# The seam into an attention layer and the attention loop: queues, banks and order of issue rewritten, with the arithmetic kept

## The chip, the core and the metric

The kernel runs on one core of a Trainium2 chip. The metric is device time in microseconds (us) of one execution. The core has a matrix engine (PE in the profile, with its weight loads shown as PEld), a vector engine (DVE), a scalar engine (ACT), a general engine (POOL) and a queue that only issues transfers and waits (SP). Matrix products land in PSUM, which has eight banks of 128 x 512 numbers in single precision; everything else lives in SBUF or in the memory outside the core, and transfers (DMAs) move between the two.

## The reference, cut to what matters

A decoder trunk of two layers over 1024 positions and 1024 features: a recurrent mixer, a feed-forward layer, stick-breaking attention with 16 heads of 64, a second feed-forward layer, and norms between them. The change touches the end of the first feed-forward layer, the norm before attention, and attention itself:

```python
def rms_norm(x, g):
    y = xf * lax.rsqrt(jnp.mean(xf * xf, axis=-1, keepdims=True) + RMS_EPS)
...
def stick_breaking_attention(x, w_qkv, w_o):
    qkv = jnp.einsum("bsd,de->bse", x, w_qkv).reshape(bsz, seq, 3, N_HEADS, HEAD_DIM)
...
        z = jnp.einsum("bhqd,bhkd->bhqk", qb, kb) * scale
        strict = s_idx < t_idx
        log_fail = jnp.where(strict, jax.nn.log_sigmoid(-z), 0.0)
        suffix = lax.cumsum(log_fail, axis=3, reverse=True) - log_fail
        weights = jnp.where(strict, jnp.exp(jax.nn.log_sigmoid(z) + suffix), 0.0)
        outs.append(jnp.einsum("bhqk,bhkd->bhqd", weights, vb))
...
    return jnp.einsum("bse,ed->bsd", o, w_o)
```

A weight of attention is thus sigmoid(z) times the product of sigmoid(-z) over all later keys up to the query, which the kernel forms with a scan along the row instead of logarithms and sums.

## The kernel before, in words

Every large product is made of three matmuls (`mm3`, L141 to L143): both operands are split into a high part in a rounded format and a low part, and high x high, high x low and low x high are added up in PSUM.

**The seam.** The last stage of the feed-forward layer visits output rows d in the order of `VISITS`. The last two visits finish the row pairs (3, 7) and (0, 4). For each finished row and half n of the positions, `finished` (L1035) stores h, calls `prep` (L214: the high part on ACT, the low part on DVE) and `squares` (L207: a square on ACT, an add onto `rbc[n]` on DVE). Then attention starts: the first q projection runs on PE, while `stats` turns the sums of squares into columns with matmuls, `rstd` makes factors of them (one ACT square root, five small DVE operations) and `broadcast_r` spreads these over a PSUM bank, which DVE copies to `rbc[n]`.

**The projections.** `qkv_steps(q)` is a generator. For pair of heads q it makes three projections (`which` 0 to 2 for q, k, v) of two halves n with eight `mm3` each, and gives control back after each `mm3`. A finished group is multiplied by `rbc[n]` on DVE (`t`, L1337). For q and k, ACT copies the high part to `qh_`, DVE makes the low part `ql_`, and SP copies the halves of these to the tiles `q`, `kh` and `kl` by transfers of 128 KB. For v, `v_turn` transposes `t` on PE in one of the two banks of `psQ` and splits it with two ACT copies and two DVE subtractions. `next_weights` splits the next projection's weights: one ACT copy of 128 x 1024 at once, and two DVE halves put on the list `later`.

**The attention loop.** Its unit is an iteration u (from -8 to 191). An iteration makes: `z_part` of chunk u + 8 (two matmuls for scores, in the two banks of `psZ`); `t_part` and `t_split` of unit u + 2 (transposes of finished weights in the two banks of `psT`, high part `th` on ACT, low part `tl` on DVE); `z_rest` of the chunk (two sigmoids on ACT, the scan on DVE, the product on POOL); one entry of `later`; two steps of the filling work (`fill`: the projections of the next pair, and after the last pair the first products with w_o into the tile `ob`); and `av_part` of unit u (two matmuls into a bank of `psO`). A head has 12 chunks: rows 0 to 7 on the diagonal (L1412), then rows 4 to 7 against the first 512 keys (L1414), whose scan starts with the last value of the diagonal's scan, kept in its tile `F4` to `F7`. A finished sum of a head is taken from PSUM by `gather`, and a pair's result is split and stored outside by `parts`; both are appended to `later`.

**What sets the order.** PE, ACT, DVE and POOL execute the order in which the code is written (`manual_schedule`). In attention the order of SP's queue is set by the framework's planner. Each engine takes its own list strictly in order, and the SP queue does too.

**The end.** After the last v projection, `all_fill` brings the stored results back from outside to `xh` and `xl` (L1495, L1496), makes the last turn of v, gives up `psQ`, opens `ob` in its place and fills in products with w_o.

Of the kernel before, what the change touches and what calls it, by code (L numbers as in the profile page):

```python
# [16 lines left out]
P = 128  # L17
# [16 lines left out]
def trunk(  # L34
# [562 lines left out]
    def mix_out_ffn_in(h, mix, bias, layer, gnext, ob):  # L597
# [124 lines left out]
        with tc.manual_schedule(engines={E.PE, E.Activation, E.DVE, E.Pool}):  # L722
# [309 lines left out]
            begun_sq = set()  # L1032
            done = []

            def finished(d, n):  # L1035
                if final:
                    squares(h, d, n, rbc, acc, first=n not in begun_sq)
                    gain(h, d, n)
                else:
                    nc.sync.dma_start(hd[d][n], h[d][n])  # L1040
                    prep(h, d, n, gnext)
                    squares(h, d, n, acc, rbc, V, first=n not in begun_sq)
                begun_sq.add(n)
# [241 lines left out]
    with ExitStack() as st:  # L1285
# [11 lines left out]
        Q, KH, KL, VV = {}, {}, {}, {}  # L1297
# [5 lines left out]
        late, later = [], []  # L1303

        def next_weights(raw):
            hi, lo = wtile("whi"), wtile("wlo")
            nc.scalar.copy(hi, raw)
            for i in range(NH):
                later.append(lambda c=half(hi, i), a=half(lo, i), b=half(raw, i): nc.vector.tensor_sub(a, b, f32(c)))
# [5 lines left out]
        def qkv_steps(q):  # L1315
            full = lambda tag: [ap.tile([P, S], F32R, tag=tag, name=tag, bufs=4) for _ in range(2)]
            VV[q] = ap.tile([P, NT, 2, P], F32R, tag="v", name="v", bufs=2)
            for which in range(3):
                w = wq.pop((q, which))
                nx = (q, which + 1) if which < 2 else (q + 1, 0)  # L1320
                if nx[0] < NP:
                    wq[nx] = next_weights(load_raw(cols(w_qkv, nx[1] * D + nx[0] * P), (ND,)))
                else:
                    mix[0].load(0)
                    mix[0].w[mix[0].order[0]] = next_weights(mix[0].raw.pop(0))
                    mix[0].load(1)
                    mix[0].load(2)
                for n in range(NH):
                    ps = psQ.tile([P, NB], F32, tag="qk", name="qk_ps")
                    for k in range(ND):  # L1330
                        mm3(ps, w[0][:, k], w[1][:, k], xh[k][n], xl[k][n], k == 0, k == ND - 1)
                        if k == 3 and late:
                            late.pop()()
                        if k < ND - 1:
                            yield
                    t = ap.tile([P, NB], F32, tag="t", name="t", bufs=2)
                    nc.vector.tensor_mul(t, ps, rbc[n])  # L1337
                    cs = slice(n * NB, (n + 1) * NB)
                    if which == 0 and n == 0:
                        Q[q] = full("q")  # L1340
                    if which == 1 and n == 0:
                        KH[q], KL[q] = full("kh"), full("kl")
                    if which < 2:
                        th = ap.tile([P, NB], F32R, tag="qh_", name="qh_", bufs=1)
                        tl = ap.tile([P, NB], F32R, tag="ql_", name="ql_", bufs=1)
                        nc.scalar.copy(th, t)
                        nc.vector.tensor_sub(tl, t, f32(th))
                        move = lambda dst, p0, src, p1: nc.sync.dma_start(f32(dst)[p0, cs], f32(src)[p1])
                        for hx, (a, b) in enumerate(((top, bot), (bot, top))):
                            if which == 0:  # L1350
                                move(Q[q][hx], a, th, a)
                                move(Q[q][hx], b, tl, a)
                            else:
                                for dst, src in ((KH[q][hx], th), (KL[q][hx], tl)):
                                    move(dst, top, src, a)
                                    move(dst, bot, src, a)
                    else:

                        def v_turn(n=n, t=t):
                            tp = psQ.tile([P, NB], F32, tag="qk", name="vt_ps")  # L1360
                            for i in range(4):
                                nc.tensor.transpose(tp[:, i * P : (i + 1) * P], t[:, i * P : (i + 1) * P], ident)
                            src = tp.rearrange("p (b h c) -> p b h c", b=4, h=2)
                            bs = slice(4 * n, 4 * n + 4)
                            for hx in range(2):
                                nc.scalar.copy(VV[q][:, bs, hx, 0:HD], src[:, :, hx])
                                nc.vector.tensor_sub(
                                    VV[q][:, bs, hx, HD:P], src[:, :, hx], f32(VV[q])[:, bs, hx, 0:HD]
                                )

                        late.append(v_turn)
                    yield
# [9 lines left out]
        F_ = {}  # L1382

        def z_part(q, hx, j, ci, c0, c1, diag):
# [3 lines left out]
            nc.tensor.matmul(ps[:, 0 : c1 - c0], lhsT=lhsT, rhs=KH[q][hx][:, c0:c1], start=True, stop=False)  # L1388
            nc.tensor.matmul(ps[:, 0 : c1 - c0], lhsT=lhsT, rhs=KL[q][hx][:, c0:c1], start=False, stop=True)  # L1389
# [202 lines left out]
```

## Time and profile before

| what | value |
|---|---|
| median of three runs | 2208.05 us (2204.42 to 2208.51) |
| the profiled execution's own time | 2209.81 us |
| its span, from first to last instruction | 2207.9 us |
| granted PE clock, mean over the span | 0.994 |
| the seam and attention in the span | from about 957 to about 1479 us |
| one pair of heads in the loop | about 60.5 us |

The profile is one execution. Its tables give busy time by engine, groups of equal instructions, what ended each idle time, and stretches of the span with the clock granted to PE. A start time is counted in us from the first instruction. The end of a matmul is modelled, so consecutive matmuls overlap in the records; the spacing of their starts tells the true pace.

### The profile page before, as it was taken

To read this page: it belongs to the slowest core of one execution; us is meant where nothing else is said; L and a number is where in the kernel's file an instruction comes from. 1 tells how busy PE (TensorE), PEld (TensorE's weight loads), DVE (VectorE), ACT (ScalarE), POOL (GpSimd) and SP (SyncE) were. 2 spreads that over 40 slices of the span, in tenths; PEclk is the share of its full clock that TensorE was granted. 3 is DMA by queue.
4 is the path that set the end of the run, shared out by engine and by line. 5 is a ranking of instruction groups with operands and counts; after the bars stand their busy time and mean duration, and the time that the engine had idled before them with its cause. 6 is when DMAs were issued, how large, how long until landed. Compare 5 with 4: busy or idle time off the path is not lost.

```text
span 2207.9 us, 28478 instructions
## 1 busy us (share of the span) xinstructions
PE 2176.5 (99%) x10120; PEld 1805.7 (82%) x10120; DVE 1709.9 (77%) x2383; ACT 1150.2 (52%) x2007; POOL 287.2 (13%) x379
## 2 busy tenths in 40 slices
PE   7999999999999999999999999989999999999998
PEld 6888888888888888878888888878888888888887
DVE  6887778767777887878888888876876777788876
ACT  5577435343444544546666666653533444454556
POOL 2222020000000000003334333321000000000002
PEclk9999999999999999999999999989999999999999
DMA  7111412334444764444333333532133444467442
GB/s 230 48 48 39 134 39 72 102 123 158 143 149 134 261 209 122 148 136 98 89 94 96 105 87 104 177 128 70 39 110 124 148 148 133 154 225 234 137 152 86
DMA packets 298702, 277.72 MB, mean 126 GB/s; under 512 B 16312, under 2 KB 215104, under 8 KB 298560
## 3 DMA queue, kind: packets, MB, share of 16 engines
q1 hardware_dynamic: 298544, 275.91, 40.1%
q8 instruction: 79, 1.29, 0.2%
q14 instruction: 63, 0.52, 0.1%
q10 hardware_dynamic: 16, 0.00, 0.0%
HBM read 175.71 MB, written 74.97 MB: 114 GB/s over the span
## 4 chain that ended last, share of the span: by engine, by line
PE 88%; DVE 6%; ACT 3%; DMA 1%; issue 1%; SPq 1%; DVEq 0%; ACTq 0%
PE p_ps L143 18%; PE p_ps L141 18%; PE p_ps L142 18%; PE qk_ps L143 3%; PE qk_ps L141 3%; PE qk_ps L142 3%; PE wt_ps L1426 3%; PE ob_ps L142 2%; PE ob_ps L141 2%; PE ob_ps L143 2%; PE a_ps L143 2%; PE a_ps L142 2%; PE a_ps L141 2%; PE z_ps L1388 1%; DVE F L1414 1%; PE z_ps L1389 1%
## 5 line engine op out<-in xcount | busy, mean ns | idle before, releaser
L1415 POOL TENSOR_TENSOR w<-w,F 128x128 f32<-128x128 f32 (+1 forms) x192 | 183.7, 957 | 311.1 <-DVE F L1412 159.0
L143 PE MATMUL p_ps<-vh,wcl 128*128 128x512 f32 x524 | 204.2, 390 | 0.5 <-DVE wcl L682 0.5
L143 PE MATMUL p_ps<-vh,wbl 128*128 128x512 f32 x524 | 204.4, 390 | 0.3 <-DVE wbl L672 0.2
L143 PE MATMUL p_ps<-vh,wal 128*128 128x512 f32 x524 | 204.1, 389 | 0.1
L141 PE MATMUL p_ps<-vh,wbh 128*128 128x512 f32 x524 | 204.2, 390 | 0.0
L141 PE MATMUL p_ps<-vh,wch 128*128 128x512 f32 x524 | 204.1, 389 | 0.0
L142 PE MATMUL p_ps<-vl,wbh 128*128 128x512 f32 x524 | 203.9, 389 | 0.0
L142 PE MATMUL p_ps<-vl,wch 128*128 128x512 f32 x524 | 203.9, 389 | 0.0
L141 PE MATMUL p_ps<-vh,wah 128*128 128x512 f32 x524 | 203.9, 389 | 0.0
L142 PE MATMUL p_ps<-vl,wah 128*128 128x512 f32 x524 | 203.9, 389 | 0.0
L668 ACT CAST wbh<-sb 128x1024 fp32r<-128x1024 f32 (+2 forms) x69 | 69.6, 1009 | 193.7 <-DVE sb L652 193.6
L212 POOL TENSOR_TENSOR acc<-acc,rbc 128x512 f32<-128x512 f32 x30 | 40.4, 1348 | 773.6 <-ACT rbc L211 773.6
L1436 DVE TENSOR_TENSOR tl<-wt_ps,th 128x512 fp32r<-128x512 f32 x192 | 106.0, 552 | 39.2 <-ACT th L1435 37.1
L1435 ACT CAST th<-wt_ps 128x512 fp32r<-128x512 f32 x192 | 92.5, 482 | 83.1 <-PE wt_ps L1426 82.0
L141 PE MATMUL qk_ps<-vh,whi 128*128 128x512 f32 x264 | 118.6, 449 | 0.7 <-ACT vh L215 0.7
L143 PEld LDWEIGHTS p_ps<-vh,wbl 128*128 128x128 f32 x524 | 98.3, 188 | 22.3 <-DVE wbl L672 2.0
L143 PEld LDWEIGHTS p_ps<-vh,wcl 128*128 128x128 f32 x524 | 98.4, 188 | 21.9 <-DVE wcl L682 1.6
L143 PEld LDWEIGHTS p_ps<-vh,wal 128*128 128x128 f32 x524 | 98.4, 188 | 21.3 <-DVE wal L663 1.0
L142 PEld LDWEIGHTS p_ps<-vl,wah 128*128 128x128 f32 x524 | 98.4, 188 | 20.6
L142 PEld LDWEIGHTS p_ps<-vl,wch 128*128 128x128 f32 x524 | 98.4, 188 | 20.5
L142 PEld LDWEIGHTS p_ps<-vl,wbh 128*128 128x128 f32 x524 | 98.4, 188 | 20.5
L141 PEld LDWEIGHTS p_ps<-vh,wbh 128*128 128x128 f32 x524 | 98.4, 188 | 20.3 <-ACT ta L1053 0.2
(400 smaller groups left out, 5851.2 us busy)
## 6 DMA issues: line engine op xcount, KB each, us to landing
raw<-in_ffn_w_in SPq DMA_DIRECT2D x88, 512.0 KB, 3.8
vl<-pd SPq DMA_DIRECT2D x128, 256.0 KB, 3.6
pd<-U SPq DMA_DIRECT2D x90, 256.0 KB, 2.3
raw<-in_ffn_w_out SPq DMA_DIRECT2D x56, 256.0 KB, 3.9
raw<-in_attn_w_qkv SPq DMA_DIRECT2D x24, 512.0 KB, 3.8
raw<-in_lru_w_in SPq DMA_DIRECT2D x16, 512.0 KB, 4.1
acc<-pd SPq DMA_DIRECT2D x28, 256.0 KB, 2.6
pph<-rbc SPq DMA_DIRECT2D x28, 256.0 KB, 2.5
```

What stands on the lines that cost most here:

```text
L141: nc.tensor.matmul(ps, lhsT=wh, rhs=mh, start=first, stop=False, **kw)
L142: nc.tensor.matmul(ps, lhsT=wh, rhs=ml, start=False, stop=False, **kw)
L143: nc.tensor.matmul(ps, lhsT=wl, rhs=mh, start=False, stop=last, **kw)
L212: (eng or nc.gpsimd).tensor_add(acc[n], acc[n], sq)
L668: nc.scalar.copy(self.full(self.wb), self.full(self.sb))
L1388: nc.tensor.matmul(ps[:, 0 : c1 - c0], lhsT=lhsT, rhs=KH[q][hx][:, c0:c1], start=True, stop=False)
L1389: nc.tensor.matmul(ps[:, 0 : c1 - c0], lhsT=lhsT, rhs=KL[q][hx][:, c0:c1], start=False, stop=True)
L1414: nc.vector.tensor_tensor_scan(rev, rev, rev, first, op0=ALU.mult, op1=ALU.bypass)
L1415: nc.gpsimd.tensor_mul(wt, wt, F[:, 1 : n + 1])
L1426: nc.tensor.transpose(tp[:, c : c + P], W[q, hx, j, kb // 4][:, (kb % 4) * P : (kb % 4 + 1) * P], ident)
L1435: nc.scalar.copy(th[:, q0:], tp[:, q0:])
L1436: nc.vector.tensor_sub(tl[:, q0:], tp[:, q0:], f32(th)[:, q0:])
```

## The change

PE, DVE, ACT and POOL keep their arithmetic; PE has the same number of matmuls. What differs is order, buffers and transfers:

1. The squares of the rows of the last two visits (eight of them) leave `finished` and follow, sorted by half, behind the last `prep`.
2. The first two q groups accumulate in `psZ` banks, take the rows in the order 1, 5, 2, 6, 3, 7, 0, 4, and are evacuated only after the factors are there. `stats` and `broadcast_r` stand at fixed steps, and the loop starts after 34 steps of projection instead of 32.
3. A k or q group's two parts lie in one tile `two` (two buffers); kh and kl become one tile `kk`, so a k group needs four transfers of 256 KB instead of eight of 128 KB. The multiplication by `rbc` stays at the end of the group; the split and the transfers follow one step later.
4. Weights are loaded one projection earlier, and split by halves on ACT too.
5. SP's queue follows the written order in attention.
6. `gather` goes to the head of `later`. The value that the scan of a later chunk starts with is copied by POOL to a column `sofar`, and all `F` tiles share four buffers.
7. The last turn of v uses a bank of `psT`; the stored results of half 0 of six pairs are brought back eight steps earlier; two steps without work are dropped before `ob`.
8. In two iterations near the end one chunk more is made, so the loop then runs two chunks further ahead.

```diff
@@ the end of the feed-forward layer
+                    if d in (VISITS[-1][0], VISITS[-2][0], VISITS[-1][0] + HK, VISITS[-2][0] + HK):
+                        last_sq.append((d, n))
+                    else:
+                        squares(h, d, n, acc, rbc, V, first=n not in begun_sq)
...
+            last_sq.sort(key=lambda t: t[1])
+            for k, (d, n) in enumerate(last_sq):
+                nc.scalar.square(acc[k % NH], h[d][n])
+                V.tensor_add(rbc[n], rbc[n], acc[k % NH])
@@ weights
-            nc.scalar.copy(hi, raw)
-            for i in range(NH):
-                later.append(lambda c=half(hi, i), a=half(lo, i), b=half(raw, i): nc.vector.tensor_sub(a, b, f32(c)))
+            part_hi = lambda i: nc.scalar.copy(half(hi, i), half(raw, i))
+            part_lo = lambda i: nc.vector.tensor_sub(half(lo, i), half(raw, i), f32(half(hi, i)))
+            def second():
+                part_lo(0)
+                part_hi(1)
+            later.extend((lambda: part_hi(0), second, lambda: part_lo(1)))
@@ qkv_steps
+                ks = (1, 5, 2, 6, 3, 7, 0, 4) if (q, which) == (0, 0) else range(ND)
+                    pool, tag = (psZ, "z") if (q, which) == (0, 0) else (psQ, "qk")
...
+                    ev = evacuate(q, which, n, ps)
+                    if (q, which) == (0, 0):
+                        waiting.append(ev)
+                        yield
+                    else:
+                        next(ev)
+                        yield
+                        next(ev, None)
@@ evacuate
+                two = ap.tile([P, 2, NB], F32R, tag="two", name="two", bufs=2)
+                nc.scalar.copy(two[:, 0], t)
+                nc.vector.tensor_sub(two[:, 1], t, f32(two)[:, 0])
...
+                        for half_ in (top, bot):
+                            nc.sync.dma_start(f32(KK[q][hx])[half_, :, cs], f32(two)[a])
...
+                pool, tag = (psT, "T") if (q, n) == (NP - 1, 1) else (psQ, "qk")
...
+            if q == NP - 1 and n == 0:
+                bring_back(*((p, 0) for p in range(NP - 2)))
@@ chunks
-            F = ap.tile([P, (n if tag != "F" else NB) + 32], F32, tag=tag, name=tag, bufs=1 if tag != "F" else 3)
+            F = ap.tile([P, NB + 32], F32, tag="F", name="F", bufs=4)
-                first = F_[j][:, 0:1]
+                first = sofar[j]
...
+            if diag and j >= 4:
+                nc.gpsimd.tensor_copy(sofar[j], F[:, 0:1])
-            later.append(gather)
+            later.insert(0, gather)
@@ the driving loops
-        with tc.manual_schedule(engines={E.PE, E.Activation, E.DVE, E.Pool}):
+        with tc.manual_schedule(engines={E.PE, E.Activation, E.DVE, E.Pool, E.SP}):
+            between = {
+                12: lambda: stats(rbc[0], psO, "o", 0),
+                16: lambda: stats(rbc[1], psO, "o", 1),
+                17: lambda: broadcast_r(psO, "o", 0),
+                18: lambda: [*waiting[0]],
+                21: lambda: broadcast_r(psO, "o", 1),
+                22: lambda: [*waiting[1]],
+            }
+            for i in range(1, 2 * ND * NH + 3):
+                next(first)
+                if i in between:
+                    between[i]()
+                if i > 4 and later:
+                    later.pop(0)()
+            gains = (len(units) - 28, len(units) - 26)
...
+                if u in gains:
+                    z_rest(z_part(*chunks[c]), *chunks[c])
+                    c += 1
```

More of the change, by code (lines that the diff above doesn't have):

```diff
@@ L1333, in qkv_steps @@
                             late.pop()()
-                        if k < ND - 1:
+                        if i < ND - 1:
                             yield
[L1336 to L1356, printed above, removed]
-                    else:
[L1359 to L1371, printed above, removed]
```

108 lines of the change are left out of this document (63 added, 45 removed).

## The prediction, as it was put on record

> **What bounds the kernel now.** I read the page first, then PE's waits, then stretches of the span, then single instructions around each wait.
>
> ```profile
> PE 2176.5 (99%) x10120; PEld 1805.7 (82%) x10120; DVE 1709.9 (77%) x2383; ACT 1150.2 (52%) x2007; POOL 287.2 (13%) x379
> PE 88%; DVE 6%; ACT 3%; DMA 1%; issue 1%; SPq 1%; DVEq 0%; ACTq 0%
> ```
>
> PE is busy almost throughout and carries 88% of the chain that ended last. The change leaves PE's work as it is, so it can only win where PE stops. PE's waits between 940 and 1480 us:
>
> ```profile
> PE ob L141 <- issue: 3.9, 1, 3.9
> PE wt_ps L1426 <- DVE tl L1436: 2.7, 2, 1.6
> PE z_ps L1388 <- ACT w L1409: 2.5, 7, 0.4
> PE qk_ps L142 <- DVE vl L216: 0.7, 1, 0.7
> PE qk_ps L141 <- ACT vh L215: 0.7, 1, 0.7
> PE p_ps L143 <- DVE wcl L682: 0.5, 1, 0.5
> PE p_ps L141 <- ACT ta L1053: 0.4, 1, 0.4
> ```
>
> That is 11.4 us in 14 stops: the last four rows are the seam, the third the loop, the first two the end of attention. A stop costs more than its idle time. The stretches, with PE, PEld, DVE, ACT and POOL busy, then PE's clock:
>
> ```profile
> 965.50:970.30 4.80, 3.48 (x15) 2.28 (x13) 4.80 (x9) 4.59 (x7) 0.00 (x0) 1.00 0.78 247
> 970.30:974.90 4.60, 4.60 (x20) 3.78 (x19) 2.39 (x9) 0.45 (x2) 0.69 (x3) 0.63 0.01 4
> 1072.00:1133.00 61.00, 60.63 (x324) 50.97 (x323) 51.53 (x75) 40.51 (x99) 23.74 (x40) 1.00 0.36 96
> 1439.80:1446.00 6.20, 6.20 (x21) 5.28 (x22) 4.86 (x5) 3.52 (x10) 1.09 (x1) 0.52 0.68 192
> 1446.00:1466.80 20.80, 20.80 (x119) 17.82 (x118) 17.83 (x24) 16.17 (x42) 9.59 (x19) 1.00 0.09 27
> 1470.60:1477.00 6.40, 6.40 (x25) 5.34 (x26) 3.09 (x6) 2.38 (x4) 0.80 (x1) 0.54 0.00 0
> 1434.00:1479.00 45.00, 38.38 (x190) 31.78 (x189) 35.75 (x47) 28.46 (x69) 15.53 (x25) 0.85 0.27 89
> ```
>
> After each group of stops the clock is low for 4.6, 6.2 and 6.4 us, at 0.63, 0.52 and 0.54. That loses 4.6 x 0.37 = 1.7, 6.2 x 0.48 = 3.0 and 6.4 x 0.46 = 2.9 us. Besides, the records hide a piece of each stop, since the end of a matmul is modelled:
>
> ```profile
> 1083.66 0.39 PE L142 MATMUL qk_ps<-vl,whi 128*128 128x512 f32 x1
> 1083.88 0.39 PE L143 MATMUL qk_ps<-vh,wlo 128*128 128x512 f32 x1
> 1084.11 0.34 PE L1447 MATMUL av_ps<-th,v 128*128 128x384 f32 x1
> 1084.28 0.34 PE L1448 MATMUL av_ps<-tl,v 128*128 128x384 f32 x1
> 1084.99 0.44 PE L1388 MATMUL z_ps<-kh,q 128*128 128x384 f32 x1 [0.37 <-ACT w L1409]
> ```
>
> A matmul of 512 columns is followed after 0.23 us, one of 384 after 0.17. Here the next starts after 0.71: 0.54 late, for an idle time of 0.37. So each stop costs 0.17 more than its row says.
>
> The rule of the Trainium skill on this ("TensorE: Matmul & The Clock Gate", Part 1) is that the clock halves after an idle window of about 3.4 us. By it the 0.7 us stops of the seam would slow nothing, and the sum below would be 1.7 smaller; the trace has 0.63 right behind them, so I go by the trace.
>
> **Part A, the seam (edits 1, 2).** PE waits because DVE is late with the last low parts:
>
> ```profile
> 968.54 0.69 DVE L212 TENSOR_TENSOR rbc<-rbc,acc 128x512 f32<-128x512 f32 x1
> 969.14 0.75 DVE L216 SCALAR_TENSOR_TENSOR vl<-h,vc,vh 128x512 fp32r<-128x512 f32 x1
> 969.95 0.50 PE L142 MATMUL qk_ps<-vl,whi 128*128 128x512 f32 x1 [0.67 <-DVE vl L216]
> ```
>
> An add of squares takes 0.60 from start to start. Eight of them, 4.8 us, no longer stand between the last h rows and their low parts; they follow, and so do eight squares on ACT. The rows 0 and 4, ready last, are used last: 18 matmuls or 4.1 us into the group. The sums are first needed by the statistics after 12 steps, 36 x 0.23 = 8.3 us, so the moved 4.8 us has cover on DVE. Between statistics of a half and its broadcast lie 5 steps, 3.4 us; the chain of six small operations fits, barely. Removed: 0.7 + 0.7 + 0.5 + 0.4 = 2.3, 4 x 0.17 = 0.7, and the slow clock's 1.7: **-4.7 us**. If that cover is too thin, the stops return at the statistics and A is worth 0; I take -4.7, because every moved piece has more room than its length.
>
> **The transfers (edits 3, 4, 5).** The rows of the K copies, and two rows of a size near the new ones:
>
> ```profile
> 990.46 1.10 SPq L1348 DMA_DIRECT2D kh<-qh__7720 x2
> 992.89 1.23 SPq L1348 DMA_DIRECT2D kh<-qh__7720 x2
> 998.23 1.05 ACT L1307 CAST whi<-raw 128x1024 fp32r<-128x1024 f32 x1
> 989.81 0.62 ACT L1346 CAST qh__7720<-t 128x512 fp32r<-128x512 f32 x1 [3.78 <-DVE t L1337]
> ```
>
> An issue costs SP about 0.6 us; 16 groups of K save four each, 38 us of a queue that is no bound. In written order K copies may stand behind stores of results and weight loads. A pair takes 61 us for 24 iterations, 2.5 each; from the end of half 0 of K to the pair's first chunk lie 5 iterations, 12.7 us, against eight issues (4.9 us) and a landing. Only in the first pair is it tight (10 steps, 6.9 us, for 2.0 of evacuation, as much again of the q group ahead, and the issues), and there the kernel before is tight too. I count 0; without that cover it is up to 1 us, once. Halving the copies on ACT costs 2 x 0.62 - 1.05 = 0.19 each, 4.6 us for 24 weights, under ACT's idle 61.0 - 40.5 a pair.
>
> **Part B, the loop (edits 3, 6).** The scores wait for their bank because ACT, in order, sits on a q copy:
>
> ```profile
> 1083.70 0.62 ACT L1346 CAST qh__8813<-t 128x512 fp32r<-128x512 f32 x1 [3.28 <-DVE t L1337]
> 1084.66 0.28 ACT L1409 ACTIVATE w<-z_ps 128x128 f32<-128x128 f32 x1
> ```
>
> ACT idles 3.28 us for `t`, and the sigmoids that free the bank stand behind it. In the change the copy comes one step later, behind the next iteration's sigmoids. Seven stops: 2.5 + 7 x 0.17 = **-3.7 us**. The least is 0, if another late operation takes its place; I take all, because the named cause goes. The 64 new copies of one column on POOL lie between a fill of one column and a copy of 128:
>
> ```profile
> L1400 POOL MEMSET F<- 128x1 f32 x128 | 12.5, 97 | 0.0
> L1296 POOL COPY unit<-ident 128x128 f32<-128x128 f32 x1 | 0.3, 289 | 0.0
> ```
>
> That is 6 to 19 us on POOL, nearer the first by width, under 61.0 - 23.7 idle us a pair: 0.
>
> **Part C, the end (edits 7, 8).** The long wait of `ob` ends with the last subtraction of v's turn, whose bank `ob` takes over; the tail's waits end with `tl` behind a scan:
>
> ```profile
> 1438.87 0.37 ACT L1366 CAST v<-vt_ps 128x256 fp32r<-128x256 f32 x1 [1.45 <-DVE v L1367]
> 1439.27 0.42 DVE L1367 TENSOR_TENSOR v<-vt_ps,v 128x256 fp32r<-128x256 f32 x1 [0.44 <-ACT v L1366]
> 1439.80 0.76 PE L141 MATMUL ob<-vh,whi 128*128 128x512 f32 x1 [3.91 <-issue]
> ...
> 1467.97 1.09 POOL L1415 TENSOR_TENSOR w<-w,F 128x512 f32<-128x512 f32 x1 [1.25 <-DVE F L1414]
> 1468.16 1.97 DVE L1414 TENSOR_TENSOR_SCAN F<-F,F 128x512 f32<-128x512 f32 x1
> 1470.60 1.33 PE L1426 MATMUL wt_ps<-ident,w 128*128 128x128 f32 x4 [1.62 <-DVE tl L1436]
> L1414 DVE TENSOR_TENSOR_SCAN F<-F,F 128x512 f32<-128x512 f32 x8 | 12.4, 1556 | 0.6 <-POOL w L1415 0.2 <-ACT F L1408 0.2
> ```
>
> With the turn in a `psT` bank, `ob` waits for no copy of v, and it may start in the iteration of the turn. What is late next: the transposes two units on need that `psT` bank, 5 us later, when the subtractions are through. But the two stops cannot be taken off whole, since DVE is nearly as full as PE. From 1434 to 1479 PE needs 38.4 - 3.0 - 2.9 = 32.5 us at full clock. DVE is busy for 35.75 of 45; two of the eight L1414 scans (2 x 1.56 = 3.1) move ahead into the loop, where DVE has 61.0 - 51.5 idle us a pair; 32.6 remain. To this I add the DVE idle time of a stretch without stops, 20.8 - 17.8 = 3.0: 35.6. So 45 - 35.6 = 9.4 are saved, less four score matmuls run earlier (0.9): **-8.5 us**. At the most DVE runs without a gap: -11.5. At the least its gaps stay: 3.1 - 0.9 = -2.2. I take the middle value, because it is measured in the same code.
>
> **The sum.** -4.7 - 3.7 - 8.5 = -16.9 us. The profiled execution took 2209.8, 1.8 above the median, so I forecast 2192.9 by the profile, **2191 us** beside the median. The forecast's own range is 2185 (C at most is 2188, and 3 more for stops that no row shows) to 2198.
>
> **The rivals.**
>
> *The tail stays DVE's.* The turn's bank delays the transposes, the extra chunks only move scans, and the slow clock returns. For it: DVE 35.75 against 32.5 of PE. Against it: DVE is free in the loop. A and B stay, C is -2.2: 2209.8 - 10.6 - 1.8 = 2197.
>
> *The seam's stops move* to the statistics: the change doesn't do there what it says. For it: six dependent operations in 3.4 us. Against it: nothing else is left on DVE then. 12.2 saved, 2196.
>
> *Slower: POOL's products land on the scans in every group of later chunks.* The scan at 1468.16 began inside POOL's product and took 1.97; with two inputs in SBUF, and 64 more POOL operations, more may. Four such scans are 7.9 us, the four `tl` up to 2.0, and the pair's weight halves, gather, t, split and v turn about 4, 13.9 in four iterations of 2.5: 3.8 behind. Two units of lead are 5 us; it decides from 1.3 more. Then one of two heads stops for 1.3 + 0.17, eight times, 11.8; B is gone and C is -2.2: -4.7 - 2.2 + 11.8 = +4.9, 2213. Against it: the loop's scans gained nothing to collide with but short copies.
>
> The Trainium skill ("SBUF — State Buffer", SBUF: two separate sides) says that DVE with two SBUF inputs and POOL take one port pair as an exclusive lock, which speaks for this rival. The trace agrees: 1.97 for the scan at 1468.16 against 1.56 in the mean.
>
> *Nothing:* each stop is replaced by another as long, 2208.
>
> **How the numbers follow.** Forecast 0.55, tail 0.17, seam 0.10, slower 0.13, nothing 0.05. A measurement of this kernel can't tell 0.2%, 4.4 us, from no change. Faster: 0.55 + 0.17 + 0.10 = 0.82; same 0.05; slower 0.13. The range reaches to 2204, past the tail case, and leaves the last two out.
>
> **What would show it.** A: no wait on `vl`, `vh`, `wcl`, `ta`, and clock 1.00 through the first q groups. B: no wait of the scores on ACT. C: no wait of `ob`, DVE near 90% busy from there to the end of attention, and a clock above 0.9. The forecast is wrong if PE waits for `tl` each pair, if the first scores wait more than 1 us for K, or if waits appear in the statistics.

## The result and the profile after

The changed kernel takes 2195.35 us (median of four executions, 2194.88 to 2196.53); beside them the kernel before took 2207.64 us (four, 2204.42 to 2208.51). The ratio is 0.9948, with a 95% interval of 0.9931 to 0.9965: 12.3 us faster by the medians. The forecast was 2191 us, with a range of 2185 to 2204. The profiled executions lie 14.3 us apart (spans of 2207.9 and 2193.6 us); the profiled execution of the kernel before, 2209.8 us, was 1.8 to 2.2 above its medians.

The page of the changed kernel: busy time of the engines, then the chain of work that ended last.

```profile
PE 2167.9 (99%) x10120; PEld 1803.3 (82%) x10120; DVE 1711.4 (78%) x2383; ACT 1155.4 (53%) x2031; POOL 315.7 (14%) x443
PE 95%; DVE 2%; ACT 1%; DMA 1%; SPq 0%; issue 0%; DVEq 0%; ACTq 0%
```

PE executes the same 10120 matmuls and now carries 95% of the chain in place of 88%. Its waits between 930 and 1470 us (us in total, times, longest):

```profile
PE wt_ps L1465 <- DVE v L1406: 2.5, 1, 2.5
PE wt_ps L1465 <- DVE tl L1475: 2.5, 2, 1.4
PE vt_ps L1401 <- DVE tl L1475: 1.2, 1, 1.2
PE z_ps L1427 <- issue: 1.1, 1, 1.1
```

Fourteen stops of 11.4 us have become five of 7.3. All waits of the seam and of the loop are gone, and so is `ob`'s wait. Three rows are new: the first scores (they wait for K's transfers, as the run with two more steps ahead of them bears out below), v's last turn, and the transposes behind it.

Where the 14.3 us of span went can be read from matmuls that both kernels execute. First in the kernel before, then in the changed one: a mark well ahead of the seam (the same matmul of the feed-forward layer, the 3825th of PE's records in both), then the av matmuls that begin unit 0, unit 156 and unit 168 of the loop, then the last of attention. (Unit 168 begins the last pair of heads.)

```profile
870.79 0.39 PE L143 MATMUL p_ps<-vh,wal 128*128 128x512 f32 x1
1012.17 0.40 PE L1447 MATMUL av_ps<-th,v 128*128 128x512 f32 x1
1404.55 0.39 PE L1447 MATMUL av_ps<-th,v 128*128 128x512 f32 x1
1432.89 0.48 PE L1447 MATMUL av_ps<-th,v 128*128 128x512 f32 x1
1478.78 0.41 PE L1448 MATMUL av_ps<-tl,v 128*128 128x512 f32 x1
```

```profile
869.62 0.39 PE L143 MATMUL p_ps<-vh,wal 128*128 128x512 f32 x1
1007.74 0.48 PE L1486 MATMUL av_ps<-th,v 128*128 128x512 f32 x1
1395.10 0.39 PE L1486 MATMUL av_ps<-th,v 128*128 128x512 f32 x1
1425.59 0.40 PE L1486 MATMUL av_ps<-th,v 128*128 128x512 f32 x1
1465.15 0.40 PE L1487 MATMUL av_ps<-tl,v 128*128 128x512 f32 x1
```

| stretch | before | after | difference | forecast |
|---|---|---|---|---|
| ahead: to the mark | 870.79 | 869.62 | -1.2 | 0 |
| seam: mark to unit 0 | 141.38 | 138.12 | -3.3 | A: -4.7, transfers 0 |
| loop: unit 0 to 156 | 392.38 | 387.36 | -5.0 | B: -3.7 |
| end: unit 156 to the last | 74.23 | 70.05 | -4.2 | C: -8.5 |
| behind attention | 729.1 | 728.4 | -0.6 | 0 |

The code of the first and the last line is the same in both kernels, so their 1.8 us belong to the two executions and not to the change. The three lines between make 12.5 us, which is what the medians say too (12.3).

Some work changed its line without being saved. Because the loop starts two steps of projection later, the seam now holds six projection matmuls and the four transposes of a turn of v more, about 1.8 us (an estimate: 6 x 0.23 + 4 x 0.11). The end has those six matmuls fewer, the loop the four transposes. With the same work on each line, the differences are about -5.1, -4.6 and -2.8 us.

The seam and the loop in stretches (length, then PE, PEld, DVE, ACT and POOL busy, PE's clock, DMA share, GB/s), in the changed kernel:

```profile
966.00:970.00 4.00, 4.00 (x19) 3.34 (x18) 3.79 (x7) 2.34 (x5) 0.00 (x0) 1.00 0.35 131
970.00:975.00 5.00, 5.00 (x32) 4.39 (x30) 3.36 (x10) 3.16 (x5) 0.69 (x3) 1.00 0.00 0
1072.00:1133.00 61.00, 61.00 (x330) 51.66 (x329) 52.67 (x76) 41.83 (x105) 27.57 (x49) 1.00 0.36 96
```

PE doesn't stop there, and the clock is 1.00 where it was 0.63. The end, from unit 156 to 168 and from 168 to the last matmul of attention, first in the kernel before, then in the changed one:

```profile
1404.55:1432.89 28.34, 28.34 (x155) 24.08 (x154) 24.34 (x36) 18.84 (x47) 10.62 (x19) 1.00 0.78 235
1432.89:1478.78 45.89, 39.27 (x195) 32.46 (x194) 36.75 (x49) 29.24 (x71) 16.41 (x25) 0.85 0.29 97
```

```profile
1395.10:1425.59 30.49, 29.34 (x160) 24.72 (x159) 26.76 (x36) 22.24 (x56) 16.18 (x27) 1.00 0.80 241
1425.59:1465.15 39.56, 34.54 (x182) 29.11 (x181) 34.31 (x46) 25.15 (x61) 18.21 (x27) 0.91 0.34 115
```

The second stretch is 6.3 us shorter and the first 2.2 us longer. Four score matmuls (0.9 us) were moved into the first, three matmuls of `ob` and a turn of v's transposes too, and six projection matmuls left it; and PE now stops in it for 1.15 us, ahead of v's turn. The slow clock is back in part: the second stretch has a mean of 0.91 in place of 0.85, and PE still idles 5.0 of its 39.56 us. DVE shows why:

```profile
1421.46 0.67 DVE L1374 TENSOR_TENSOR t<-qk_ps,rbc 128x512 f32<-128x512 f32 x1
1422.04 1.85 DVE L1451 TENSOR_TENSOR_SCAN F<-F,sofar 128x512 f32<-128x512 f32 x1
1423.82 0.53 DVE L1475 TENSOR_TENSOR tl<-wt_ps,th 128x384 fp32r<-128x384 f32 x1
1424.27 1.97 DVE L1451 TENSOR_TENSOR_SCAN F<-F,sofar 128x512 f32<-128x512 f32 x1
1426.16 0.39 DVE L1475 TENSOR_TENSOR tl<-wt_ps,th 128x256 fp32r<-128x256 f32 x1
1426.48 2.10 DVE L1451 TENSOR_TENSOR_SCAN F<-F,sofar 128x512 f32<-128x512 f32 x1
...
1430.20 0.42 DVE L1406 TENSOR_TENSOR v<-vt_ps,v 128x256 fp32r<-128x256 f32 x1 [0.44 <-ACT v L1405]
```

DVE works through this list without a gap until v's first half is done. The turn's transposes were finished by 1425.1, and its last subtraction ends at 1430.6, behind two scans. The transposes of a later unit want the turn's `psT` bank before that, and wait 2.55 us for it.

### The profile page after: what moved, and what is told of

It reads as the page before. It is cut to its first block, busy times and chain, and to the rows that moved or that the text cites. A ratio compares the mean times of both kernels' runs of the same rounds, so it can differ in the third digit from the quotient of the medians.

```text
span 2193.6 us, 28494 instructions
## 1 busy us (share of the span) xinstructions
PE 2167.9 (99%) x10120; PEld 1803.3 (82%) x10120; DVE 1711.4 (78%) x2383; ACT 1155.4 (53%) x2031; POOL 315.7 (14%) x443
## 4 chain that ended last, share of the span: by engine, by line
PE 95%; DVE 2%; ACT 1%; DMA 1%; SPq 0%; issue 0%; DVEq 0%; ACTq 0%
PE p_ps L143 18%; PE p_ps L141 18%; PE p_ps L142 18%; PE qk_ps L143 4%; PE qk_ps L141 4%; PE qk_ps L142 4%; PE wt_ps L1465 3%; PE ob_ps L141 2%; PE ob_ps L142 2%; PE ob_ps L143 2%; PE a_ps L141 2%; PE a_ps L142 2%; PE a_ps L143 2%; PE z_ps L1427 2%; PE z_ps L1428 2%; PE av_ps L1487 2%
## 5 line engine op out<-in xcount | busy, mean ns | idle before, releaser
L1452 POOL TENSOR_TENSOR w<-w,F 128x128 f32<-128x128 f32 (+1 forms) x192 | 192.5, 1002 | 268.3 <-DVE F L1449 164.6
L1475 DVE TENSOR_TENSOR tl<-wt_ps,th 128x512 fp32r<-128x512 f32 x192 | 105.6, 550 | 48.9 <-ACT th L1474 46.9
L1449 DVE TENSOR_TENSOR_SCAN F<-F,unit 128x128 f32<-128x128 f32 (+3 forms) x128 | 115.4, 902 | 2.8 <-ACT F L1445 2.6
L141 PEld LDWEIGHTS p_ps<-vh,wch 128*128 128x128 f32 x524 | 98.4, 188 | 20.8 <-ACT tb L1057 0.5
L141 PEld LDWEIGHTS p_ps<-vh,wah 128*128 128x128 f32 x524 | 98.4, 188 | 20.4
```

Source lines behind the costliest of these rows:

```text
L141: nc.tensor.matmul(ps, lhsT=wh, rhs=mh, start=first, stop=False, **kw)
L1449: nc.vector.tensor_tensor_scan(rev, rev, unit[:, NB - n :][:, ::-1], first, op0=ALU.mult, op1=ALU.add)
L1452: nc.gpsimd.tensor_mul(wt, wt, F[:, 1 : n + 1])
L1475: nc.vector.tensor_sub(tl[:, q0:], tp[:, q0:], f32(th)[:, q0:])
```

## The experiments

Two measures serve below. "The stretch" of the expectations runs from the last projection matmul to the last av matmul: 1420.00 to 1465.15, 45.2 us, in the changed kernel. It suits runs that share the order of the projections, but not the kernel before (47.2), in which the projections end one iteration later against the units. "From unit 156" is the line "end" of the table, 70.05 us. All edits are to the changed kernel. The first eight runs and that of the whole old end were executed once each (beside the first eight, the kernel before took 2206.5 and 2206.8 us), so they are read by stretches of the trace and not by their total. Two of them change only the seam; their stretch is 44.7 and 44.8 us in place of 45.2, so half a microsecond in this measure says nothing.

### The bank of v's last turn

```diff
-                pool, tag = (psT, "T") if (q, n) == (NP - 1, 1) else (psQ, "qk")
+                pool, tag = psQ, "qk"
```

> The last turn of v goes back into the bank that `ob` takes over; all else as in the changed kernel, where the last projection matmul and the last matmul of the attention output lie 45.2 us apart, with three stops of PE behind v's turn (1.15, 2.55 and 1.05 + 1.42 in the tail). Theory (VectorE is behind there, and the bank only chooses who waits for it): `ob` waits 3 to 5 us instead of the transposes, and the stretch is 44.5 to 47.5 us. Rival (the choice of the psT bank makes the stops): without it 1.15 + 2.55, their 2 x 0.17 and the slow clock behind them (5 us at 0.66, 1.7 us) go, and the stretch is 40 to 42 us.

Measured: 2198.33 us, a stretch of 48.9 us, and `ob` waits 7.0 us, as PE's waits between 1400 and 1470 us show:

```profile
PE ob L141 <- issue: 7.0, 1, 7.0
PE wt_ps L1465 <- DVE tl L1475: 2.7, 3, 1.4
```

The rival is out: the `psT` bank doesn't make the stops; with `ob` right behind the turn it saves 3.7 us. The theory fell short as well, since it matters who waits: one stop of 7.0 us stands in place of 1.15 and 2.55. `ob` is the next thing in PE's order behind the turn, the transposes that want the `psT` bank come later.

### The two chunks ahead

```diff
-            gains = (len(units) - 28, len(units) - 26)
+            gains = ()
```

> The two chunks that run ahead are taken out (edit 8 undone). Theory (the end is bound by VectorE, so what is moved ahead of it is won): two scans of 1.8 us come back into the tail, less the four score matmuls (0.9 us) that went ahead: the stretch from the last projection matmul to the end of attention grows from 45.2 to 47.7 to 49.7 us, and PE's waits for `tl` in the tail (2.5 us in two stops) grow to 5 or more. Rival (the stops come from the turn alone): only the 0.9 us comes back, 45.5 to 46.5 us, with the same two stops.

Measured: 2197.44 us, a stretch of 47.5 us and four stops for `tl` of 4.5 us in all. Both come just short of the theory's numbers (47.7, and 5 or more) and are far from the rival's. From unit 156, where both versions hold the same matmuls, it is 72.0 us: the two chunks are worth 1.9 us together, about the time of one scan and not of two.

### The second half of an evacuation one step later

```diff
                         next(ev)
-                        yield
                         next(ev, None)
+                        yield
```

> The second half of an evacuation (copy to hi, subtraction, transfers) is given out right behind the product again, not one step later (edit 6 undone); the K tiles and the order of the queue stay. Theory (ACT sat on the q copy): PE's scores wait for `w` of ACT again once in each pair, 0.37 us and 0.17 beside, and a pair of heads takes 60.2 to 60.4 us where it took 59.65. Rival (the two tiles and the transfers in written order removed the stops): no such wait, 59.5 to 59.75 us a pair.

Measured: 2198.91 us; unit 0 to 156 (1007.60 to 1397.57) takes 390.0 us in place of 387.4, and a pair 59.8 to 60.1 us. (What is undone is a part of edit 3.) PE's own rows show no wait. Those of its weight loads do, for instance

```profile
1077.68 0.19 PEld L1427 LDWEIGHTS z_ps<-kk,q 128*128 128x128 f32 x1 [0.44 <-ACT w L1446]
```

This is the stop on `w`, with its matmul starting 0.17 us late and the next ones up to 0.1 each. So the cause is the theory's, at a smaller size: 0.4 us a pair, below its 60.2 to 60.4 us and above the rival's range, and not all of the 0.75 that a pair gained. The K tiles, the split of the weights by halves and the order of the queue were not undone alone.

### The squares in line again

```diff
-                    if d in (VISITS[-1][0], VISITS[-2][0], VISITS[-1][0] + HK, VISITS[-2][0] + HK):
+                    if False:
```

> The last squares are taken in line again, not at the end (edit 1 undone), while the group of q keeps the order that uses rows 0 and 4 last. Theory (VectorE's and ACT's squares made the operands late): PE waits for `wcl` and `ta` again (0.5 + 0.4 us) and for `vl` or `vh` (up to 1.4 us), the clock falls to about 0.63 behind them, and the first scores come 2.5 to 4.5 us later than 990.4. Rival (the order of the rows did it): no wait for `vl` or `vh`, clock 1.00, first scores 0.5 to 1.5 us later.

Measured: 2196.57 us. The waits for `wcl` (0.5) and `ta` (0.4) are back, those for `vl` and `vh` are not, and the clock stays at 1.00. The first scores come at 991.4, and 1.7 us later than in the changed kernel when both are counted from the mark. The rival's mechanism holds (its range ended at 1.5): squares and order of rows remove different stops. From the 400th record before the q group to the group it is 93.0 us in place of 91.3: two stops of 0.95 us idle in all cost 1.7.

### The rows of the first q group in the old order

```diff
-                ks = (1, 5, 2, 6, 3, 7, 0, 4) if (q, which) == (0, 0) else range(ND)
+                ks = range(ND)
```

> The first q group uses its rows in the order 0 to 7 again; the squares stay at the end. Theory (it is the order that keeps `vl` and `vh` off the path, the squares only `wcl` and `ta`): PE waits for `vl` or `vh` of rows 0 and 4, 0.3 to 1.4 us idle in one to four stops, and the first scores come 0.5 to 2.5 us later after the last matmul of the layer before than the 28.3 us of the changed kernel. Rival (with the squares away the low parts are in time in any order): no such wait, 28.2 to 28.5 us.

Measured: 2197.8 us; the first scores follow the last matmul of the layer before after 29.7 us in place of 28.3, and one wait is back. The stretch with that stop and the stretch behind it:

```profile
967.20 0.50 PE L142 MATMUL qk_ps<-vl,whi 128*128 128x512 f32 x1 [0.67 <-DVE vl L216]
...
966.00:970.00 4.00, 3.30 (x13) 2.49 (x14) 3.79 (x7) 2.51 (x5) 0.00 (x0) 1.00 0.56 197
970.00:975.00 5.00, 5.00 (x28) 4.28 (x27) 4.09 (x11) 3.78 (x6) 0.69 (x3) 1.00 0.00 0
```

The theory holds. One stop of 0.67 us costs 1.3 and leaves the clock alone. The two edits cost 1.7 and 1.3 us alone; together the kernel before lost more by the second stop of the q group (0.7) and the slow clock (1.7).

### The products of the last pair on DVE

```diff
-            nc.gpsimd.tensor_mul(wt, wt, F[:, 1 : n + 1])
+            (nc.gpsimd if diag or q < NP - 1 else nc.vector).tensor_mul(wt, wt, F[:, 1 : n + 1])
```

> For the last pair of heads the product behind each later scan (8 of them with 512 columns for each head is 8 in all for the pair, 4 a head) is made by VectorE instead of POOL. Theory (a scan is long because it runs beside POOL's product: 1.28 us alone, 1.85 to 2.12 beside it): these 8 scans fall from a mean of 1.79 to 1.25 to 1.40 us, VectorE pays 0.7 for each product, nothing is won or lost in its sum, and the stretch from the last projection matmul to the end of attention stays at 45.2 us within 1.5. Rival (the scans are long by themselves, or for another transfer): they stay near 1.8, VectorE has 5.6 us more to do, and the stretch grows to 48 to 51 us.

Measured: 2198.69 us, a stretch of 47.6 us. The groups of DVE between 1419 and 1466 us (count, busy us, mean ns), first the changed kernel, then this one:

```profile
L1451 DVE TENSOR_TENSOR_SCAN F<-F,sofar 128x512 f32<-128x512 f32 x8 | 14.4, 1794 | 0.0
```

```profile
L1451 DVE TENSOR_TENSOR_SCAN F<-F,sofar 128x512 f32<-128x512 f32 x8 | 10.9, 1368 | 0.0
L1452 DVE TENSOR_TENSOR w<-w,F 128x512 f32<-128x512 f32 x8 | 5.5, 692 | 0.8
```

The scans fall by 0.43 us each: POOL's products beside them cost DVE 3.5 us in the tail. The price on DVE, 5.5 us, is 2.0 more than that, and the stretch grows by 2.5, which was outside the theory's 1.5. So the mechanism holds, and POOL remains the better place.

### The weight split later, and two iterations without a chunk

```diff
             qs.close()
-            mix[0].proc(1)
...
                 for k in range(ND - 1):
+                    if i == 0 and k == 2:
+                        mix[0].w[mix[0].order[1]] = next_weights(mix[0].raw.pop(1))
```

> The second weight of the output projection is split (1.05 us on ACT, 1.23 on VectorE, whole, in the iteration of v's last turn) two matmul groups of `ob` later and in halves. Theory (VectorE's order in that one iteration is too full): the 0.5 wait and the 1.23 us leave it, the next `tl` (before at 12.3 us after the last projection matmul) comes 1.2 to 1.8 us sooner, and the stretch falls from 45.2 to 43.4 to 44.4 us; the 2.55 us stop, which ends before that split, stays. Rival (VectorE's sum bounds the whole end): the same work comes later, 44.8 to 45.4 us.

Measured: 2195.77 us, a stretch of 44.9 us: the rival, within what runs with an equal end differ by. What leaves DVE's list at the turn comes back as stops for `tl` (3.3 us in place of 2.5).

The next run adds two iterations without a chunk:

```diff
+            hold.extend((0, 0))
             yield
             yield
             late.pop()()
...
-                some = chunks[c : c + 1]
-                c += 1
+                some = [] if hold else chunks[c : c + 1]
+                c += 0 if hold else 1
+                hold[:1] = []
```

> As the run with the weight split later, and the two iterations around v's last turn take no new chunk: the two chunks that ran ahead are spent there. Theory (PE stops because v's subtractions stand behind two scans of 2 us on VectorE): the stops of 1.15 and 2.55 us shrink to 1.2 or less together, the clock stays at 1.00 behind them, and the stretch falls to 40.5 to 43 us. Rival (VectorE's sum bounds the end, its order does not matter): the two scans come back in the tail, where the stops for `tl` grow from 2.5 us to 5 or more, and the stretch is 44 to 46 us.

Measured: 2197.27 us, a stretch of 46.3 us. PE's waits between 1400 and 1470 us:

```profile
PE wt_ps L1465 <- DVE tl L1475: 3.6, 4, 1.3
PE vt_ps L1401 <- DVE tl L1475: 1.6, 1, 1.6
PE wt_ps L1465 <- POOL w L1452: 0.6, 1, 0.6
PE wt_ps L1465 <- DVE v L1406: 0.3, 1, 0.3
```

The wait behind v fell from 2.55 to 0.3 us, as wanted, and the time was given back in the tail. The rival is nearer, though its numbers missed too (46.3 us against 44 to 46, 3.6 us for `tl` against 5 or more): the order of DVE's list moves the stops about and doesn't remove them.

### Four chunks ahead

```diff
-            wt = ap.tile([P, n], F32, tag=tag, name=tag, bufs=1 if diag else 4)
+            wt = ap.tile([P, n], F32, tag=tag, name=tag, bufs=1 if diag else 5)
...
-            gains = (len(units) - 28, len(units) - 26)
+            gains = (100, 130, 162, 164)
```

> The changed kernel with four chunks ahead at the end in place of two: one more taken in the iterations 100, 130, 162 and 164 each, and a fifth buffer for the `w` of the later chunks. Theory (VectorE's sum bounds the end, and it has idle time in the loop): two more scans leave the tail, as the first two were worth 1.9 us in all, so the stretch from the last projection matmul to the end of attention falls from 45.2 to 42 to 43.8 us, the loop grows by the 0.9 us of four score matmuls alone, and the time is 2193 to 2194.5 us against 2195.35. Rival (the loop has no room, or the `w` buffers come free too late): PE stops in the iterations with two chunks or in the tail for a bank or buffer, the stretch stays above 44.5 us, and the time is 2195 us or more.

Measured: 2200.08 us (median of five, 2199.16 to 2203.35; ratio to the kernel before 0.9965, interval 0.9951 to 0.9978): slower than the changed kernel. From unit 156 it is 68.1 us, 2.0 less than 70.05, and the stretch falls to 40.2 us, further than the theory's 42 to 43.8, so its account of the end holds. But unit 0 to 156 takes 395.0 us, 7.7 more, of which the score matmuls explain 0.9. (This is the slowest of the five executions, 3.3 us above their median.) PE's waits, and two of the waiting matmuls:

```profile
PE z_ps L1427 <- DMA kk<-two: 5.4, 4, 2.9
...
1344.03 0.55 PE L1427 MATMUL z_ps<-kk,q 128*128 128x256 f32 x1 [2.91 <-DMA kk<-two]
1356.70 0.35 PE L1427 MATMUL z_ps<-kk,q 128*128 128x256 f32 x1 [0.43 <-DMA kk<-two]
```

The first chunks on each half of K of the later pairs now came one or two iterations sooner, before K had landed. Behind the stop of 2.91 us the clock is 0.50 from 1343.21 to 1350.03, which loses another 3.4 us: with 3.3 us idle in the loop and the 0.9 of the score matmuls that is 7.6 of the 7.7. Neither theory had this.

### The whole old end

```diff
-                pool, tag = (psT, "T") if (q, n) == (NP - 1, 1) else (psQ, "qk")
+                pool, tag = psQ, "qk"
...
-            later.insert(0, gather)
+            later.append(gather)
...
             mix.append(ob)
+            for _ in range(2):
+                yield
...
-            gains = (len(units) - 28, len(units) - 26)
+            gains = ()
```

> The end as it was before the change, all else as in the changed kernel: v's last turn in the bank that `ob` takes over, one iteration (two steps) between the turn and `ob`, no chunks ahead, the gathers at the end of the list. With the turn's bank alone undone the stretch from the last projection matmul to the end of attention was 48.9 us, with the chunks alone 47.5, in the changed kernel 45.2, in the kernel before 47.2. Theory (bank, step and chunks work together, and the iteration between turn and `ob` did most of what the bank does now): the stretch is 46.7 to 47.7 us as before, and `ob` waits 3 to 5 us. Rival (another edit, the 64 copies on POOL and the shared tiles, made the end longer and ate a part of the gain): 49 to 51 us, with longer scans than the 1.56 us of before.

Measured: 2203.14 us, a stretch of 48.0 us, between both; `ob` waits 4.2 us as the theory said, and the scans have a mean of 1.74 us as the rival said (1.56 before). From unit 156 it is 72.5 us, 1.8 less than in the kernel before, of which 1.4 are the six projection matmuls that run in the seam now. So the other edits left the end about as long as it was; what they save and cost there was not taken apart. The run showed something else. Unit 0 to 156 (1008.34 to 1399.80) takes 391.5 us, 4.1 more than in the changed kernel, with six waits like

```profile
1138.53 0.50 PE L1486 MATMUL av_ps<-th,v 128*128 128x512 f32 x1 [0.42 <-DVE oo L1497]
```

Of this run's edits only the place of `gather` acts in the loop. At the end of the list it is late, and the next head's first av matmul waits for its bank. The kernel before had it there too, without this stop; its list held two entries for each weight where there are three now, which would explain it, but that was not tried.

### K's transfers at the first scores, and the best version

```diff
-            for i in range(1, 2 * ND * NH + 3):
+            for i in range(1, 2 * ND * NH + 5):
```

> The changed kernel with two more projection steps (1.4 us of PE) ahead of the first scores, nothing else. Theory (the wait for K's transfers there, 1.06 us idle and some 0.4 beside, is time lost): it goes, the first scores come at most 0.3 us later with two steps more done, and the run takes 2193.7 to 2194.8 us where the changed kernel took 2195.35. Rival (an iteration more behind the projections, where VectorE is the bound, gives it back): the stretch behind the last projection matmul grows by 0.8 us or more, and the run takes 2195 to 2196.5 us.

Measured: 2194.04 us (median of four, 2193.20 to 2195.27; ratio to the kernel before 0.9938, interval 0.9914 to 0.9962). The stop is gone; the first scores come 0.1 us later after the layer before, with 1.4 us of projection more behind them; the stretch grows by 0.4. The theory's window holds and the rival's does not, but the executions overlap with those of the changed kernel by 0.4 us, so the gain of 1.3 us is likely rather than settled.

The last run joins this with the weight split later and the four chunks ahead; one iteration more of projection also gives K time to land.

> As the run with four chunks ahead, with the split of the output projection's second weight later and in halves, and with two more projection steps (1.4 us of PE) ahead of the first scores, which wait 1.1 us for K's transfers in the changed kernel. Theory (the stop is time lost: 1.06 idle, 0.17 hidden, some 0.2 behind it): the stop goes, the first scores come at most 0.3 us later with two steps more done, and the run is 0.8 to 1.8 us shorter than the one with four chunks ahead alone. Rival (an iteration taken from the loop, which PE bounds, comes back in the tail, which VectorE bounds): the stretch behind the last projection matmul grows by 1 to 2.5 us, and both runs agree within 0.7 us.

Measured: 2192.46 us (median of five, 2191.64 to 2193.51; ratio to the kernel before 0.9931, interval 0.9919 to 0.9944). It is 2.9 us faster than the changed kernel, with no execution in common: the fastest version here. No matmul waits for `kk`; from unit 156 it is 64.7 us. Against the run with four chunks it is 7.6 us shorter, not 0.8 to 1.8. In the traces the loop is 6.6 us shorter, which is the K wait and the slow clock behind it; neither theory had them. The rival's other sign came true: the stretch behind the last projection matmul grew by 1.8 us, from 40.2 to 42.0. The end is now DVE's more than ever, busy 38.24 of 42.10 us, and PE's clock is 1.00:

```profile
1418.80:1460.90 42.10, 37.24 (x208) 29.92 (x208) 38.24 (x51) 28.66 (x70) 21.69 (x30) 1.00 0.39 136
```

## Why the prediction was right, and where it was not

**Sign and sum.** The sum was -16.9 us. The part of the trace that the change touches gives -12.5, and the medians -12.3. PE's time was won where PE stopped, as forecast: the stops of the seam and of the loop went for the reasons given. The end went another way than its sum supposed. That the total is only 4 us off is in part luck: A and B were worth more than they were priced at, which made up for some of C.

**Part A, right in cause: -3.3 us in place of -4.7.** All four stops are gone and the clock is 1.00 through the first q groups. But 1.8 us of work from the loop and the end moved into this stretch, which the prediction didn't count, and the change added a stop that it counted at 0, "up to 1 us, once": the first scores wait 1.05 us for K. A wait of more than 1 us there was one of its own signs of being wrong, and it came true, barely. So what was removed is worth about 6 us (3.3 + 1.8 + 1.05, an estimate; one of the loop's seven stops, 0.32 us, is in it). A short stop costs more than the 0.17 us beside its row: 1.7 us for two of 0.95 idle in all, 1.3 for one of 0.67. The statistics took the moved squares without a stop.

**The transfers, right by luck of one iteration.** In the loop nothing waits, as said. But the "12.7 us" were set against issues and a landing without a price, and without the evacuation ahead of them. The median landing of the copies around the first scores is 4.2 us (first row, transfers by issue). In the loop half 0 of a K group is multiplied at 1331.79 and its first copy issued at 1334.67 (timeline of the changed kernel):

```profile
kk<-two SPq DMA_DIRECT2D x8, 256.0 KB, 4.2
```

```profile
1331.79 0.68 DVE L1374 TENSOR_TENSOR t<-qk_ps,rbc 128x512 f32<-128x512 f32 x1
...
1334.67 11.43 SPq L1391 DMA_DIRECT2D kk<-two  x6
```

The pair's first scores start at 1343.1. Of 11.3 us, 2.9 go to the evacuation and some 4 to 6 to issues and landing, which leaves about one iteration of 2.5 us (an estimate from these rows). Asking for a chunk one or two iterations sooner made PE wait up to 2.9 us. The changed kernel is safe because both its extra chunks are made in the last pair, after its first scores.

**Part B, right in cause, too small.** -5.0 us over the 13 heads in the table (-4.6 with the moved transposes set aside) against -3.7. A stop of 0.37 idle was priced at 0.54, by the start of the waiting matmul. A pair won 0.75: the starts behind each stop were late too (scores to scores 0.10, scores to transposes 0.08), and so was an av pair some 10 us ahead of it (0.08). And "the named cause goes" was not enough of a reason. With the step between product and copy taken away (edit 3), a pair loses 0.4; with `gather` at the end of the list (edit 6), it loses 0.6 on another wait. The prediction put no price on the second. The 64 copies on POOL took 22.4 us where it had 6 to 19: their median is 0.18 us, but the longest, beside a scan, took 1.12. POOL had room for it, so the 0 stands.

**Part C, mis-sized: -4.2 us in place of -8.5.** The failed step is "To this I add the DVE idle time of a stretch without stops, 20.8 - 17.8 = 3.0". That idle time belonged to 20.8 us, and was added once to 32.6 us of work. As a share, 17.83 of 20.80 is 86% busy, and the end would have needed 32.6 / 0.857 = 38.0 us in place of 35.6. The measured share from unit 168 on is 34.31 of 39.56, 87%, with 5.25 us idle: 2.3 us of the 4.3 missing. A further 0.7: DVE's busy time fell by 2.4 us, not by 3.1, as the scans became longer (1.56 to 1.79 us in the mean): seven of the eight now begin beside a product of POOL, in the kernel before five. The last 1.3 lies ahead of unit 168, mostly in the stop of 1.15 us at v's turn. The prediction saw that the transposes need the turn's bank "5 us later, when the subtractions are through"; the subtractions were through 5.6 us after the turn's transposes, and the bank was asked for 2.4 us before that. Of the 4.2 us that the end did win, 1.4 are the projection matmuls that moved into the seam.

The rival "the tail stays DVE's" was thus right about the mechanism, and -2.2 is near the -2.8 us that remain without the moved matmuls; it had named the slow clock's return as well, and its 2197 us lies nearer to the measured 2195.35 than the forecast's 2191. The end is bound by DVE's work and the share of it that can be packed: moving work inside the list changed nothing (0.3 us) or lost 1.2, and taking two scans out of the end won 1.9, two more 2.0. The *slower* rival named a real cost, POOL's products beside the scans (0.43 us each in the tail), in a place where it didn't decide: in the loop PE has no stop at all.

The Trainium skill ("SBUF — State Buffer", SBUF: two separate sides) has DVE with two inputs in SBUF and a POOL operation that reads SBUF take one port pair in turn. The trace agrees: the scans of the last pair take 1.79 us in the mean with POOL's products and 1.37 without. Scan by scan, in the changed kernel, one that meets no product takes 1.28 us, and the others take 1.08 us more than they overlap with a product (overlaps of 0.77, 0.89 and 1.04 us: 1.85, 1.97 and 2.12).

## What to carry to other kernels

When an engine is the next bound, carry its busy share over from a stretch without stops, not its idle microseconds, and expect its own instructions to lengthen where more of them meet another engine's. Compare two traces at a matmul that is the same in both, and count the work on each side of it: here 1.2 us of start-up and 1.8 us of moved matmuls would have passed for the change. A removed wait has a successor: undo each edit alone, for here two edits held off two different stops, and leaving either out gave back 0.4 or 0.6 of the 0.75 us a pair. Work taken ahead must be checked against when its operands land, not when their transfers are issued.

## What was not expected of the hardware

A short stop of PE costs about twice its idle row: 0.37 idle cost 0.75 a pair, two of 0.95 together cost 1.7, one of 0.67 cost 1.3. A wait may stand only in the rows of the weight loads (0.44 us there, none on the matmul), so a list of PE's waits that is empty doesn't prove that PE runs freely.

The granted clock in these traces is 1.00 or 0.50, with nothing between. The 0.63 over 4.6 us of the kernel before, behind its two stops of 0.66 and 0.67 us, is one stretch of 3.41 us at half clock, seen in a wider window:

```profile
971.32:974.73 3.41, 3.41 (x12) 2.83 (x12) 2.20 (x8) 0.20 (x1) 0.50 (x3) 0.50 0.00 0
```

The slow stretches of the seam, the loop and the end last 3.41 us or a multiple of it in every run (6.83 at the 3.91 us wait of `ob`, 10.24 at the one of 7.0). Which stops bring one is less certain. One stop of 0.67 us left the clock at 1.00. The stops of 1.15 and 2.55 us around v's turn took it down in the changed kernel; in the run with the weight split later, the same two stops, at the same times, did not. First the changed kernel, then that run:

```profile
1430.00:1435.00 5.00, 4.23 (x20) 3.84 (x21) 4.28 (x7) 4.37 (x13) 1.06 (x1) 0.66 0.86 315
1430.00:1435.00 5.00, 4.23 (x27) 3.85 (x28) 4.54 (x8) 4.83 (x15) 1.85 (x4) 1.00 0.98 367
```

So 1.7 us of slow clock (half of 3.41) can come or not with the same stop, and the 1.7 that part A put down for the seam rests on one trace of the kernel before.

The Trainium skill ("TensorE: Matmul & The Clock Gate", Part 1) speaks of an idle window of about 3.4 us before the clock halves, and its section on a second failure mode of frequent short idles that throttle it too. The stops of the seam and of v's turn are shorter than that window and were followed by half clock, so they agree with the second.
